# Second norm by halves with the sample between its pairs, first activations loaded among the up tiles, two more key/query buffers and another place for a table in the set-up

## The chip, the core and the metric

The kernel runs on one core of one Trainium2 chip. What counts is the time on the device, in microseconds (us), from the first to the last instruction and what lies around them. TensorE (PE) multiplies matrices, VectorE (DVE), ScalarE (ACT) and GpSimd (POOL) do the rest, SyncE (SP) issues most transfers (DMA). Each engine takes its own instructions strictly in their order; between engines an instruction can wait for others by semaphores.

## The reference, cut to what matters

One layer of a streaming encoder over 1024 prompt rows and 32 sample rows of width 1024, in float32.

```python
xn = rmsnorm(h, norm_mix)
proj = xn @ w_in
u_a, u_b, v_b, q, k, v, gates = jnp.split(proj, IN_SPLITS, axis=-1)
y_a = s5_mixer(u_a, ...)              # diagonal state space model
y_b = sgu_mixer(u_b, v_b, ...)        # layernorm, then a triangular 128x128 product
y_c = stick_breaking(q, k, v, ...)    # causal attention, 8 heads of 64
g = jax.nn.sigmoid(gates)
h = h + (g0 * (y_a @ w_branch_a) + g1 * (y_b @ w_branch_b) + g2 * (y_c @ w_branch_c)) @ w_out
xn2 = rmsnorm(h, norm_ffn)
gate, up = jnp.split(xn2 @ w_gate_up, 2, axis=-1)
h = h + (jax.nn.silu(gate) * up) @ w_down     # hidden width 2816
y = rmsnorm(h, norm_final)
```

## The kernel before

Each float32 factor is kept as a high and a low part (`hi`, `lo`), and a product is made of three matmuls, hi·hi, hi·lo and lo·hi (`mm3`, lines 144 to 146). The parts are made by ACT (a copy that rounds) and by POOL or DVE (the rest). The stages follow one another in the profiled execution thus: first norm, values, keys and queries and the set-up of the state space model to 170 us; the spatial gating (`sgu`) to 260; the state space model (`s5_main`) and attention to 650; gates and the output projection of half 0 to 780, gates of half 1 to 932; output projection of half 1 beside the second norm of half 0 to 999; the first two up tiles beside the second norm of half 1 to 1071; the other up tiles (22 in all, each 128 columns of gate and of up) to 1487; the down product in groups of two tiles from 1499 to the end.

A scheduler puts the instructions of each engine in order, by priorities and its own costs. Only TensorE in the part that starts with `out_proj(1, ...)` and ends with chunk 0 of up tile 1 keeps the order of the code (`tc.manual_schedule`).

The places that the change touches:

- `qk_dense` makes keys and queries of a pair of heads in pieces of 512 or 272 columns. ACT writes the high part of a piece into a buffer `qe` (L326), a copy into `k32` (L329), DVE the low part (L330), and SP stores `qe` to DRAM (L332). There are two buffers. Each key is also turned by TensorE and copied out by ACT (`kt`, L307).
- `s5_setup` builds tables; one of them, `KK`, is copied by 16 transfers into a matrix `D` (L632). `KK` lies in a buffer named `big`; the pool that holds it is closed after the set-up, and `sgu` puts its tiles in the same place, its `vb` (L377) where `big` was. So `vb` waits for the transfers.
- `out_proj(half, ...)` runs over four quarters of 256 columns and, in each, over the blocks of 128 rows; in half 1 the 32 sample rows (block 8) come last. After each second quarter ACT sums the squares of the block (L1168).
- `norm2(chunk, ...)` is a generator that stands beside other work: each `yield` lets the caller put a block or a product on TensorE. It takes the reciprocal roots of all blocks at once (`rstd_all`, thirteen small rows on DVE with the sum ahead), multiplies a block's 1024 columns by the norm's weights on POOL (L1213) and by the root on ACT (L1214), turns it on TensorE (L1202), and makes seven operands of a pair of blocks (L1221, L1222). The last, for the sample, comes after both pairs.
- `up_tile(i, ...)` takes seven products of a tile's weights and the operands. The weights are loaded (`raw`), combined and split by `up_weights` (ACT L1285; POOL or DVE L1286). The results go to `act_d`, one tensor in DRAM.
- `load_act(gr)` loads two tiles of `act_d` for a group of the down product (`ra`, L1401) and splits them (ACT L1402, POOL L1403, DVE L1404). It is called after all up tiles, and the loads of `h` (`hd0`, `hd1`) stand behind it.

Of the kernel before, what the change touches and what calls it, by code (L numbers as in the profile page):

```python
# [16 lines left out]
TP, TS = 1024, 32  # L17
# [31 lines left out]
def trunk_kernel(ctx: ExitStack, tc: tile.TileContext,  # L49
# [154 lines left out]
    with ExitStack() as ph1:  # L204
# [86 lines left out]
        def qk_dense(wk, hp):  # L291
# [22 lines left out]
            for which in (1, 0):  # L314
                unit = next_unit(768 + 512 * which + 128 * hp)
                dst = (q_d, k_d)[which][hp]
                for h, o, n, t0 in CHUNKS:
# [7 lines left out]
                    qe = wk.tile([128, 2, 512], F32R, name="qe", bufs=2)  # L325
# [95 lines left out]
        def s5_setup(pl, keep, out):  # L421
# [185 lines left out]
            KK = pl.tile([32, 8, 128], F32, name="KK", tag="big")  # L607
# [425 lines left out]

        qk_tasks = [qk_dense(qk, hp) for hp in range(4)]
        tasks.extend(qk_tasks)
        tasks.extend(gate_ahead(qk, h, m) for h in range(2) for m in range(AHEAD[h]))
        with pool("s5k", 1) as s5k:
            sgc = sgu_consts(s5k)
            with pool("s5t", 1) as s5t, pool("pv", 1) as pv:
                S = {}  # L1040
                setup = s5_setup(s5t, s5k, S)
                next(setup)
                v_dense(pv)
                next(setup)
                finish(qk_tasks[0])
                next(setup)
                finish(qk_tasks[1])
                for _ in setup:
                    pass
            with pool("sgu", 1) as sg:  # L1050
# [97 lines left out]
    def out_proj(half, mt, junk, beside=iter(())):  # L1148
        wo = w_out[0].rearrange("(k p) c -> p k c", p=128)
        for q in range(4):  # L1150
            us = tm_units(wo, 256 * q)
            for b in PAIRS[half][0] + PAIRS[half][1] + ((8,) if half else ()):
# [13 lines left out]
                if q % 2:  # L1166
                    c = slice(256 * q - 256, 256 * q + 256)
                    s.activation(junk()[0:rows], h_rows(b)[:, c], AF.Square, scale=1.0 / 32,  # L1168
                                 accum_out=ss2[0:rows, 10 * half + 5 * (q // 2) + (b % 4 if b < 8 else 4):][:, 0:1])
# [6 lines left out]
    act_d = dram.tile([FF, T], F32, name="act_d")  # L1176
# [22 lines left out]
    def turned(xb, rows, q, pt):  # L1199
        for e in range(4):  # L1200
            k = 4 * q + e
            pe.transpose(pt[:, 128 * e:128 * e + rows], xb[:, 128 * k:128 * k + 128], ident[0:rows, 0:rows])  # L1202
        return pt.rearrange("p (a b) -> p a b", b=128)[:, :, 0:rows]

    def ps_turn():
        return ps2.tile([128, 512], F32, name="ptn", tag="t2", bufs=2)

    def norm2(chunk, wk, X, gap):

        def scaled(b):  # L1210
            i, rows = b % 4 if b < 8 else 4, BLOCKS[b][1]
            xb = wk.tile([128, 1024], F32, name="xb")[0:rows]
            g.tensor_mul(xb, h_rows(b), gb[0:rows])  # L1213
            s.activation(xb, xb, AF.Copy, scale=r[0:rows, i:i + 1])  # L1214
            return xb
# [29 lines left out]
        order = [b for p in PAIRS[chunk] for b in p] + ([8] if chunk else [])  # L1245
        ss = wk.tile([128, 5], F32, name="ss5")
        v.tensor_add(ss, ss2[:, 10 * chunk:10 * chunk + 5], ss2[:, 10 * chunk + 5:10 * chunk + 10])
        r = rstd_all(wk, ss, 5)
        for j in range(2):
            xa = scaled(order[2 * j])  # L1250
            for _ in range(gap):
                yield
            x11 = turned(xa, 128, 0, ps_turn())
            x21 = turned(xa, 128, 1, ps_any())

            def second():
                xb = scaled(order[2 * j + 1])
                for _ in range(gap):
                    yield
                return [turned(xb, 128, q, ps_turn()) for q in range(2)]  # L1260

            yield from operands_of(128 * j, 128, x11, x21, second)
        if chunk:
            xs_ = scaled(8)
            sp.dma_start(h_d[chunk], H[chunk])
            for _ in range(gap):
                yield
            a0, a1 = turned(xs_, 32, 0, ps_turn()), turned(xs_, 32, 1, ps_any())
# [6 lines left out]
        else:  # L1275
            sp.dma_start(h_d[chunk], H[chunk])
# [28 lines left out]
    def up_tile(i, wk, chunks, X, weights=None, beside=iter(())):  # L1305
# [43 lines left out]
        for c in chunks:  # L1349
# [3 lines left out]
            for e, o in enumerate((sg[c], a[c])):  # L1353
                t0 = 512 * c + 256 * e
                sp.dma_start(act_d[128 * i:128 * i + 128, t0:t0 + 256], o[:, 0:256])
                if c:
                    t0 = TP + 16 * e
                    sp.dma_start(act_d[128 * i:128 * i + 128, t0:t0 + 16], o[:, 256:272])
# [6 lines left out]
    with pool("wu", 1) as wk:  # L1365
# [3 lines left out]
        NF = FF // 128  # L1369
        with tc.manual_schedule(engines={mybir.EngineType.PE}):  # L1370
            work = norm2(0, wk, X0, 2)
# [132 lines left out]
```

## Time and profile before

| | |
|---|---|
| median of 3 runs | 1771.8 us (1768.79 to 1782.83) |
| the profiled execution | 1785.0 us, its span 1783.3 us |
| TensorE busy | 1657.8 us, 93% of the span |
| DVE, ACT, POOL busy | 964.7, 603.6, 623.3 us |
| mean granted clock of TensorE | 0.964 of full speed |
| DMA | 211.57 MB, 119 GB/s over the span |

A row of a timeline gives the start and the duration of an instruction, and in brackets how long its engine stood idle ahead of it and what ended that. A row of the windows gives a stretch and the busy time of each engine in it. A granted clock of 0.50 is the lower of TensorE's two levels, 1.2 GHz, and 1.00 the upper, 2.4 GHz; a value between is a stretch with both.

### The profile page before, as it was taken

How to read it: one execution, taken by the hardware profiler on the slowest of the kernel's cores; microseconds unless marked ns; L12 is line 12 of the kernel's file. 1: busy time of each engine (PE TensorE's matmuls, PEld its weight loads, DVE VectorE, ACT ScalarE, POOL GpSimd, SP SyncE). 2: the span in 40 equal slices, each digit the busy share in tenths (PEclk: the TensorE clock that was granted, in tenths of full speed). 3: DMA queues.
4: the chain of work that ended last, by engine and by line, in shares of the span. 5: the costliest groups of instructions: out<-in, count | busy, mean ns of one | idle time of the engine just before them, and what ended most of it. 6: DMA issues, size and time to landing. Idle time of an engine off the chain costs nothing. (4 is left out here: it accounts for less than half of the span.)

```text
span 1783.3 us, 28031 instructions
## 1 busy us (share of the span) xinstructions
PE 1657.8 (93%) x10949; PEld 1502.6 (84%) x10949; DVE 964.7 (54%) x1838; ACT 603.6 (34%) x1102; POOL 623.3 (35%) x369
## 2 busy tenths in 40 slices
PE   6988999899988899999998879999999997999997
PEld 6977897677777788899998879999999996777775
DVE  7962523322699840730275656655555554765645
ACT  5322332123466632323224443333333332321114
POOL 2210221334010322534456554333333324644534
PEclk9988999699999999999999989999999998999999
DMA  7443245155766526764361222232222225422212
GB/s 222 113 128 82 85 123 132 60 161 159 190 150 163 149 78 212 242 215 143 94 206 37 98 75 66 82 98 73 73 72 79 87 88 203 145 79 90 72 36 86
DMA packets 271421, 211.57 MB, mean 119 GB/s; under 512 B 68340, under 2 KB 244504, under 8 KB 270776
## 3 DMA queue, kind: packets, MB, share of 16 engines
q1 hardware_dynamic: 242728, 194.56, 37.0%
q10 hardware_dynamic: 28560, 15.21, 2.9%
q8 instruction: 86, 1.41, 0.3%
q14 instruction: 47, 0.39, 0.1%
HBM read 153.83 MB, written 55.30 MB: 117 GB/s over the span
## 5 line engine op out<-in xcount | busy, mean ns | idle before, releaser
L118 POOL TENSOR_TENSOR wl<-raw,wh 128x1024 fp32r<-128x1024 f32 x120 | 304.6, 2544 | 747.1 <-ACT wh L117 705.9
L117 ACT ACTIVATE wh<-raw 128x1024 fp32r<-128x1024 f32 x120 | 126.5, 1057 | 320.1 <-PE p L146 151.0
L144 PE MATMUL p<-xo,wl 128*128 128x256 f32 (+1 forms) x616 | 177.2, 288 | 9.6 <-ACT xo L1221 6.3
L144 PE MATMUL p<-xo,wh 128*128 128x256 f32 (+1 forms) x616 | 178.0, 289 | 2.2 <-ACT wh L1285 2.1
L146 PE MATMUL p<-xo,wh 128*128 128x256 f32 (+1 forms) x616 | 178.1, 289 | 1.6 <-POOL wh L1286 1.6
L146 PE MATMUL p<-xo,wl 128*128 128x256 f32 (+1 forms) x616 | 177.4, 288 | 0.0
L145 PE MATMUL p<-xo,wh 128*128 128x256 f32 (+1 forms) x616 | 176.8, 287 | 0.0
L145 PE MATMUL p<-xo,wl 128*128 128x256 f32 (+1 forms) x616 | 176.4, 286 | 0.0
L144 PE MATMUL p_d<-xnh,wh 128*128 128x272 f32 (+1 forms) x464 | 157.9, 340 | 10.4 <-ACT vb L377 7.2
L146 PE MATMUL p_d<-xnh,wl 128*128 128x272 f32 (+1 forms) x464 | 155.5, 335 | 5.3 <-POOL wl L118 5.3
L145 PE MATMUL p_d<-xnl,wh 128*128 128x272 f32 (+1 forms) x464 | 155.3, 335 | 0.0
L1453 DVE TENSOR_TENSOR hd<-p,hd 128x512 f32<-128x512 f32 x160 | 107.1, 685 | 69.4 <-PE p L146 69.0
L145 PE MATMUL p<-wl,act 128*128 128x512 f32 x352 | 140.0, 398 | 2.4 <-POOL wl L118 2.4
L144 PE MATMUL p<-wh,act 128*128 128x512 f32 x352 | 139.9, 398 | 0.0
L146 PE MATMUL p<-wh,act 128*128 128x512 f32 x352 | 139.7, 397 | 0.0
L1286 POOL TENSOR_TENSOR wh<-raw,wh 128x512 fp32r<-128x512 f32 x59 | 77.6, 1317 | 147.1 <-ACT wh L1285 142.7
L1286 POOL TENSOR_TENSOR wl<-raw,wl 128x512 fp32r<-128x512 f32 x58 | 78.4, 1353 | 141.4 <-ACT wl L1285 141.4
L144 PEld LDWEIGHTS p<-xo,wl 128*128 128x128 f32 x616 | 117.7, 191 | 9.9 <-ACT xo L1221 6.4
L144 PEld LDWEIGHTS p<-xo,wh 128*128 128x128 f32 x616 | 118.4, 192 | 2.7 <-ACT wh L1285 2.3
L146 PEld LDWEIGHTS p<-xo,wh 128*128 128x128 f32 x616 | 118.1, 192 | 1.8 <-POOL wh L1286 1.8
L145 PEld LDWEIGHTS p<-xo,wh 128*128 128x128 f32 x616 | 118.7, 193 | 0.0
L145 PEld LDWEIGHTS p<-xo,wl 128*128 128x128 f32 x616 | 118.1, 192 | 0.0
(463 smaller groups left out, 4432.3 us busy)
## 6 DMA issues: line engine op xcount, KB each, us to landing
raw<-in_w_in_dram SPq DMA_DIRECT2D x66, 512.0 KB, 4.0
raw<-in_w_gate_up_dram SPq DMA_DIRECT2D x46, 512.0 KB, 4.6
ra<-act_d SPq DMA_DIRECT2D x22, 528.0 KB, 3.6
raw<-in_w_down_dram SPq DMA_DIRECT2D x22, 512.0 KB, 3.7
q<-q_d SPq DMA_DIRECT2D x64, 128.0 KB, 2.9
raw<-in_w_out_dram SPq DMA_DIRECT2D x16, 512.0 KB, 5.3
act_d<-fs SPq DMA_DIRECT2D x44, 128.0 KB, 1.7
act_d<-fa SPq DMA_DIRECT2D x44, 128.0 KB, 4.9
```

What stands on the lines that cost most here:

```text
L117: s.activation(wh, raw, AF.Copy)
L118: g.tensor_sub(wl, raw, wh.bitcast(F32))
L144: pe.matmul(ps, ah, bh, start=start, stop=False)
L145: pe.matmul(ps, ah, bl, start=False, stop=False)
L146: pe.matmul(ps, al, bh, start=False, stop=stop)
L1286: eng.tensor_sub(lo, src, hi.bitcast(F32))
L1453: v.tensor_add(hr[:, cs], ps, hr[:, cs])
```

## The change

Four edits go together.

1. While the set-up runs, `qe` comes in turn from two pools with two buffers each.
2. `KK` takes the place of the buffer `tg`, not `big`.
3. The second norm handles a block in two halves of 512 columns with two buffers. The roots are taken for each pair of blocks, in half 1 for three blocks first (the sample and the first pair). Half 1's blocks run in the order 8, 4, 6, 5, 7 in the output projection too, and the sample's operands come between the two pairs. A block is asked for three steps of TensorE ahead, and half 1's norm begins inside `out_proj`, after the third block of the last quarter.
4. `act_d` becomes 22 tensors. The first group's load stands in the loop over up tiles, after tile 19 in the code, the second's behind the loop but ahead of the down stage's pool, with the loads of `h` between.

```diff
-                    qe = wk.tile([128, 2, 512], F32R, name="qe", bufs=2)
+                    qe_turn[0] += 1
+                    qe = qe_pools[qe_turn[0] % len(qe_pools)].tile([128, 2, 512], F32R, name="qe", bufs=2)
...
-            KK = pl.tile([32, 8, 128], F32, name="KK", tag="big")
+            KK = pl.tile([32, 8, 128], F32, name="KK", tag="tg")
...
-            for b in PAIRS[half][0] + PAIRS[half][1] + ((8,) if half else ()):
+            for i, b in enumerate(ORDER[half]):
...
+                if q == 3 and i == 2:
+                    next(then, None)
...
-    act_d = dram.tile([FF, T], F32, name="act_d")
+    act_d = [dram.tile([128, T], F32, name=f"act_d{i}") for i in range(FF // 128)]
...
+    ORDER = ((0, 2, 1, 3), (8, 4, 6, 5, 7))
...
+        def roots(blocks):
+            i, n = order.index(blocks[0]), len(blocks)
+            ss = wk.tile([128, 5], F32, name="ss5", bufs=2)[:, 0:n]
+            o = 10 * chunk + i
+            v.tensor_add(ss, ss2[:, o:o + n], ss2[:, o + 5:o + 5 + n])
+            y = rstd_all(wk, ss, n)
+            for j, b in enumerate(blocks):
+                r[b] = y[:, j:j + 1]
...
-            xb = wk.tile([128, 1024], F32, name="xb")[0:rows]
-            g.tensor_mul(xb, h_rows(b), gb[0:rows])
-            s.activation(xb, xb, AF.Copy, scale=r[0:rows, i:i + 1])
+            for q in range(2):
+                c = slice(512 * q, 512 * q + 512)
+                xb = wk.tile([128, 512], F32, name="xb", tag="xh", bufs=2)[0:rows]
+                g.tensor_mul(xb, h_rows(b)[:, c], gb[0:rows, c])
+                s.activation(xb, xb, AF.Copy, scale=r[b][0:rows])
+                out.append(xb)
...
+        for j, (ba, bb) in enumerate(PAIRS[chunk]):
+            roots((8, ba, bb) if chunk and j == 0 else (ba, bb))
+            xa = scaled(ba)
+            for _ in range(3):
+                yield
...
+            yield from operands_of(128 * j, 128, x11, x21, second)
+            if chunk and j == 0:
+                yield from sample()
+        sp.dma_start(h_d[chunk], H[chunk])
...
+        with pool("wn", 1) as wn, tc.manual_schedule(engines={mybir.EngineType.PE}):
+            work, work1 = norm2(0, wn, X0), norm2(1, wn, X1)
+            out_proj(1, mB, lambda: wn.tile([128, 512], F32, name="junk2", tag="xt", bufs=2), work, work1)
...
+        with pool("wa", 1) as wa:
+            up_tile(1, wk, (1,), X, held)
+            up_tile(0, wk, (1,), X)
+            for i in range(2, FF // 128):
+                up_tile(i, wk, (0, 1), X)
+                if i == FF // 128 - 3:
+                    acts = [load_act(0, wa, hx)]
+            for half in range(2):
+                H[half] = hx.tile([128, 4, 1024], F32, name=f"hd{half}", tag="hx")
+                sp.dma_start(H[half], h_d[half])
+            acts.append(load_act(1, wa))
```

The set-up's instructions stand in the same order on all engines; what changes are the waits. On ACT, from the first `qe` of the first pair of heads on, with the semaphores that a row waits for in brackets (DMAHW are transfers; one line number less in the kernel before), the kernel before has:

```order
L326 ACTIVATE qe<-p_av 128x512 [waits PE_49]
L329 ACTIVATE k_1283<-p_av 128x512
L326 ACTIVATE qe<-p_d 128x272 [waits PE_49]
L329 ACTIVATE k_1283<-p_d 128x272
L117 ACTIVATE wh<-raw 128x1024 [waits DMAHW7_49,PE_49,Pool_49]
L326 ACTIVATE qe<-p_av 128x272 [waits DMAHW4_49,DMAHW5_49,DVE_49,PE_49]
L329 ACTIVATE k_1283<-p_av 128x272
L307 ACTIVATE kt<-p_t 128x256 [waits PE_49]
```

and the changed kernel has:

```order
L327 ACTIVATE qe<-p_av 128x512 [waits PE_49]
L330 ACTIVATE k_1283<-p_av 128x512
L327 ACTIVATE qe<-p_d 128x272 [waits PE_49]
L330 ACTIVATE k_1283<-p_d 128x272
L117 ACTIVATE wh<-raw 128x1024 [waits DMAHW7_49,PE_49,Pool_49]
L327 ACTIVATE qe<-p_av 128x272 [waits PE_49]
L330 ACTIVATE k_1283<-p_av 128x272
L307 ACTIVATE kt<-p_t 128x256 [waits PE_49]
```

The third `qe` has lost its wait for transfers and for DVE. In the same way the first `vb` of `sgu`, which waited for eight transfer semaphores and DVE, waits for nothing more in the changed kernel, and DVE's first `yt` waits for those eight.

On POOL, beside the first two up tiles, the second norm of half 1 and the tiles' weights share the engine. `xb` are blocks times the norm's weights (`h_9037` and `h_9058` are half 1 of h, `hS` the sample), `xo` are low parts of operands, `wh` and `wl` low parts of weights. Before:

```order
L1286 TENSOR_TENSOR wh<-raw,wh 128x512
L1213 TENSOR_TENSOR xb<-h_9037,gb 128x1024
L1286 TENSOR_TENSOR wl<-raw,wl 128x512 x2
L1213 TENSOR_TENSOR xb<-h_9037,gb 128x1024
L1222 TENSOR_TENSOR xo_9973<-t_10142,xo_9973 128x4x128
L1222 TENSOR_TENSOR xo_9974<-t_10146,xo_9974 128x4x128
L1286 TENSOR_TENSOR wh<-raw,wh 128x512
L1286 TENSOR_TENSOR wl<-raw,wl 128x512
L1213 TENSOR_TENSOR xb<-h_9037,gb 128x1024
L1222 TENSOR_TENSOR xo_9974<-t_10152,xo_9974 128x4x128
L1222 TENSOR_TENSOR xo_9287<-r_10077,xo_9287 128x4x128
L1286 TENSOR_TENSOR wh<-raw,wh 128x512
```

And in the changed kernel:

```order
L1309 TENSOR_TENSOR wh<-raw,wh 128x512
L1231 TENSOR_TENSOR xb<-h_9058,gb 128x512 x2
L1231 TENSOR_TENSOR xb<-hS,gb 32x512 x2
L1247 TENSOR_TENSOR xo_10045<-t_10184,xo_10045 128x4x128
L1247 TENSOR_TENSOR xo_10046<-t_10188,xo_10046 128x4x128
L1231 TENSOR_TENSOR xb<-h_9058,gb 128x512
L1247 TENSOR_TENSOR xo_10046<-t_10194,xo_10046 128x4x128
L1309 TENSOR_TENSOR wl<-raw,wl 128x512
L1247 TENSOR_TENSOR xo_9308<-r_10117,xo_9308 128x4x128
L1231 TENSOR_TENSOR xb<-h_9058,gb 128x512
L1309 TENSOR_TENSOR wl<-raw,wl 128x512
```

Blocks have become pairs of halves, the sample's stand ahead of the first pair's operands, and between two weight rows there are now eight rows for the norm.

On SP the first loads of activations stand in the changed kernel where the first tiles have just been stored (`act_d_6931` is tile 0, `act_d_6932` tile 1, and so on; the tiles' order is 1, 0, 2, 3):

```order
L1381 DMA act_d_6931<-fs 128x16
L1316 DMA raw<-in_w_gate_up_dram 128x8x128
L1378 DMA act_d_6931<-fa 128x256
L1381 DMA act_d_6931<-fa 128x16
L1316 DMA raw<-in_w_gate_up_dram 128x8x128
L1388 DMA ra<-act_d_6931 128x1056
L1388 DMA ra<-act_d_6932 128x1056
L1378 DMA act_d_6933<-fs 128x256 x2
```

Before, the first of them stood behind the last tile's last store:

```order
L1355 DMA act_d<-fa 128x256 x2
L1358 DMA act_d<-fa 128x16
L116 DMA raw<-in_w_down_dram 128x1024
L1401 DMA ra<-act_d 128x1056 x2
L1467 DMA hd_15650<-h_d_6929 128x4096
L1467 DMA hd_15652<-h_d_6930 128x4096
```

So the first group's two loads have moved from behind tile 21 to behind tile 0, and none of the other tiles' stores stands ahead of them.

## Rows read from the trace of the kernel before

**Rows 1.** The page: busy time of TensorE, share of the span, instructions

```profile
PE 1657.8 (93%) x10949; PEld 1502.6 (84%) x10949; DVE 964.7 (54%) x1838; ACT 603.6 (34%) x1102; POOL 623.3 (35%) x369
```

**Rows 2.** Waits of TensorE: for whom, us in total, times, the longest

```profile
PE p L1443 <- DVE act L1404: 12.3, 2, 11.5
PE ptn L1202 <- ACT xb L1214: 12.1, 3, 4.5
...
PE p_t L305 <- ACT kt L307: 7.0, 1, 7.0
...
PE p L144 <- DVE fs L1330: 3.3, 1, 3.3
```

**Rows 3.** Windows: stretch, its length, busy us of each engine, clock, DMA

```profile
100.00:112.00 12.00, 7.52 (x40) 7.50 (x41) 3.37 (x8) 3.15 (x9) 0.00 (x0) 0.57 0.89 223
164.00:176.00 12.00, 6.57 (x32) 6.57 (x33) 5.68 (x37) 3.74 (x16) 0.00 (x0) 0.57 0.15 28
328.00:360.00 32.00, 32.00 (x101) 24.13 (x101) 3.33 (x2) 6.56 (x10) 9.40 (x4) 0.52 0.18 50
...
950.00:1000.00 50.00, 45.49 (x379) 45.29 (x378) 25.76 (x36) 24.12 (x47) 32.99 (x19) 0.97 0.17 53
1000.00:1050.00 50.00, 31.31 (x212) 29.98 (x212) 32.07 (x59) 25.17 (x48) 34.57 (x26) 0.85 0.30 95
...
1100.00:1487.00 387.00, 387.00 (x3168) 387.00 (x3167) 225.96 (x448) 120.97 (x242) 124.45 (x93) 1.00 0.28 81
...
1487.00:1508.00 21.00, 8.73 (x26) 5.60 (x25) 6.86 (x10) 5.03 (x7) 9.59 (x5) 0.59 0.83 316
```

**Rows 4.** Timeline of ACT, DVE and SP in the set-up; DMA issues, us to landing

```profile
98.77 0.68 DVE L330 TENSOR_TENSOR qe<-k,qe 128x512 fp32r<-128x512 f32 x1
...
103.10 0.55 SPq L113 DMA_DIRECT2D raw<-in_w_in_dram  x1
...
103.47 0.40 ACT L326 ACTIVATE qe<-p_av 128x272 fp32r<-128x272 f32 x1 [12.46 <-DMA k_d<-qe]
...
112.37 1.06 ACT L117 ACTIVATE wh<-raw 128x1024 fp32r<-128x1024 f32 x1 [0.90 <-PE p_d L145]
...
raw<-in_w_in_dram SPq DMA_DIRECT2D x66, 512.0 KB, 4.0
...
k_d<-qe SPq DMA_DIRECT2D x8, 256.0 KB, 3.2
```

**Rows 5.** Timeline of SP, ACT and TensorE at the start of `sgu`

```profile
160.67 6.91 SPq L632 DMA_DIRECT2D D<-KK  x9
...
168.91 0.38 ACT L377 ACTIVATE vb<-p_d 128x256 f32<-128x256 f32 x1 [6.21 <-DMA D<-KK]
...
169.44 0.59 PE L144 MATMUL p_d<-xnh,wh 128*128 128x272 f32 x1 [7.21 <-ACT vb L377]
```

**Rows 6.** Timeline of DVE and POOL beside the first up tiles

```profile
1001.90 0.33 DVE L1247 TENSOR_TENSOR ss<-ss 128x5 f32<-128x5 f32 x1 [0.85 <-ACT junk L1168]
...
1005.80 0.17 DVE L1196 SCALAR_TENSOR_TENSOR rs_a<-rs_a 128x5 f32<-128x5 f32 x1
...
1046.19 1.26 POOL L1222 TENSOR_TENSOR xo<-r,xo 128x512 fp32r<-128x512 f32 x1 [0.26 <-ACT xo L1221]
```

**Rows 7.** Timeline of SP, POOL and TensorE at the down stage; landing of `ra`

```profile
1492.62 0.86 SPq L1401 DMA_DIRECT2D ra<-act_d  x2
...
1498.62 2.38 POOL L1403 TENSOR_TENSOR act<-ra,act 128x1024 fp32r<-128x1024 f32 x1 [7.71 <-ACT act L1402]
...
1498.83 0.69 PE L1443 MATMUL p<-wh,act 128*64 128x512 f32 x1 [11.53 <-DVE act L1404]
...
ra<-act_d SPq DMA_DIRECT2D x22, 528.0 KB, 3.6
```

**Rows 8.** Timeline of DVE: one line beside POOL's work, and alone

```profile
1014.59 1.50 DVE L1343 TENSOR_TENSOR fs<-fs,ft 128x256 f32<-128x256 f32 x1
...
1035.38 0.43 DVE L1343 TENSOR_TENSOR fs<-fs,ft 128x256 f32<-128x256 f32 x1
```

More of the change, by code (lines that the diff above doesn't have):

```diff
@@ L1049, in trunk_kernel @@
                     pass
+                qe_pools.pop()
             with pool("sgu", 1) as sg:
@@ L1146, in gates, with out_proj @@
         return mt
-    def out_proj(half, mt, junk, beside=iter(())):
+    def out_proj(half, mt, junk, beside=iter(()), then=iter(())):
         wo = w_out[0].rearrange("(k p) c -> p k c", p=128)
@@ L1243, in operands_of, with sample @@
             split(6, r11, g)
[L1245 to L1263, printed above, removed]
+        def sample():
             xs_ = scaled(8)
[L1265 to L1268, printed above, removed]
+            yield
+            yield
+            a0, a1 = turned(xs_[0], ps_turn()), turned(xs_[1], ps_any())
             def both():
@@ L1354, in up_tile, with load_act @@
                 t0 = 512 * c + 256 * e
-                sp.dma_start(act_d[128 * i:128 * i + 128, t0:t0 + 256], o[:, 0:256])
+                sp.dma_start(act_d[i][:, t0:t0 + 256], o[:, 0:256])
                 if c:
                     t0 = TP + 16 * e
-                    sp.dma_start(act_d[128 * i:128 * i + 128, t0:t0 + 16], o[:, 256:272])
+                    sp.dma_start(act_d[i][:, t0:t0 + 16], o[:, 256:272])
+    def load_act(gr, wk, p=hy):
+        act = p.tile([128, 2, 2 * T], F32R, name="act", tag="hx" if p is hx else "hy")
+        for e in range(2):
+            ra = wk.tile([128, T], F32, name="ra", tag="xb")
+            sp.dma_start(ra, act_d[2 * gr + e])
+            s.activation(act[:, e, 0:T], ra, AF.Copy)
+            g.tensor_sub(act[:, e, T + TS:2 * T], ra[:, 0:TP], act[:, e, 0:TP].bitcast(F32))
+            v.tensor_sub(act[:, e, T:T + TS], ra[:, TP:T], act[:, e, TP:T].bitcast(F32))
+        return act
     with pool("wg", 1) as wk:
@@ L1393, in trunk_kernel @@
         NG = FF // 256
-        def load_act(gr, p=hy):
-            act = p.tile([128, 2, 2 * T], F32R, name="act", tag="hx" if p is hx else "hy")
-            for e in range(2):
-                f0 = 256 * gr + 128 * e
-                ra = wk.tile([128, T], F32, name="ra", tag="xb")
-                sp.dma_start(ra, act_d[f0:f0 + 128, :])
-                s.activation(act[:, e, 0:T], ra, AF.Copy)
-                g.tensor_sub(act[:, e, T + TS:2 * T], ra[:, 0:TP], act[:, e, 0:TP].bitcast(F32))
-                v.tensor_sub(act[:, e, T:T + TS], ra[:, TP:T], act[:, e, TP:T].bitcast(F32))
-            return act
         def final_norm(b, ss):
@@ L1462, in down_groups @@
                 final_norm(*done)
-        acts = [load_act(0, hx)]
-        for half in range(2):
-            H[half] = hx.tile([128, 4, 1024], F32, name=f"hd{half}", tag="hx")
-            sp.dma_start(H[half], h_d[half])
-        acts.append(load_act(1))
         for gr in range(NG):
             if gr + 2 < NG:
-                acts.append(load_act(gr + 2))
+                acts.append(load_act(gr + 2, wk))
             if gr < NG - 2:
```

53 lines of the change are left out of this document (28 added, 25 removed).

## The prediction

> **What bounds the kernel now.** I read the page first: TensorE is busy 1657.8 of 1783.3 us [rows 1], so a change can only pay where TensorE stands still or runs at the lower clock. The view by windows shows where that isn't: in 1100 to 1487 it is busy 387.00 of 387.00 us at granted clock 1.00 [rows 3], so the twenty up tiles there can't become shorter. The waits of TensorE then give the stalls with their releasers [rows 2]. Four belong to code that the diff touches, and each ends a chain that I followed back in the timelines. After a stall the clock is low: the windows around three of them have 0.57, 0.57 and 0.59 of full clock, so half the time at the lower of the two levels, 1.2 GHz instead of 2.4 [rows 3]. I price that part as busy time times (1 - clock): 7.52 x 0.43 = 3.2 us, 6.57 x 0.43 = 2.8 us, 8.73 x 0.41 = 3.6 us.
>
> The profiled execution took 1785.0 us (span 1783.3 plus 1.7 around it), 13.2 above the median of the three runs, 1771.8. One stretch could explain it: from 328 to 360 TensorE is fully busy at 0.52 [rows 3], 32 x 0.48 = 15.4 us more than at full clock. Nothing in the diff is there; the other two runs have no trace, so this is a guess. I take the saving from 1785.0 and then shift it by -13.2.
>
> **Part A, four buffers for keys and queries: 5 us.** TensorE waits 7.0 us for ACT's `kt` [rows 2]. ACT was stuck 12.46 us at the third `qe` until 103.47, behind the first buffer's store; that buffer was finished by DVE only at 98.77, between rows of the S5 set-up, and a store of it takes 3.2 us [rows 4]. With four buffers the third and fourth need no wait, as the order shows. The third could then run when TensorE is done, some 6 to 7 us earlier. What is late next: `raw`, issued on SP at 103.10 behind the stores, which still wait for DVE; with 4.0 us to land it is there at 107.1, and ACT's `wh` from it, now at 112.37, can come 112.37 - 107.1 = 5.3 us earlier at most [rows 4]. ACT's copies of the S5 table stand behind that `wh`, and TensorE's PSUM behind those. So the bounds are 0 (all of it turns into this wait) and 7.0 + 3.2 = 10.2; I take 5, since the `wh` is the last link. More buffers add no instruction.
>
> **Part B, the set-up table KK in another place: 8.5 us.** ACT stood 6.21 us at `vb` until 168.91, for the transfers out of KK; TensorE waited 7.21 and restarted at 169.44. The nine last transfers are issued from 160.67 over 6.91 us [rows 5]. The order shows `vb` without a wait now; the sixteen transfers are waited for at DVE's first `yt`, behind the normalisation. Gain: 6.2 plus 2.8 of clock = 9.0, less 0.5 for what the normalisation still waits for. Bounds: 5 (the normalisation, DVE and ACT in turn, is the next bound) and 9.5.
>
> **Part C, second norm in halves, sample between the pairs: 18 us.** TensorE stands still 50 - 45.49 = 4.51 us in 950 to 1000 and 50 - 31.31 = 18.69 in 1000 to 1050, 23.2 in all; by clock 0.97 and 0.85 another 1.4 + 4.7 = 6.1 [rows 3]. Three waits for `xb` alone hold 12.1 [rows 2].
> The halves cost nothing: POOL's 1024 elements take 2.38, its 512 take 1.26 [rows 6, 7], so two halves are 0.14 more, but the first half leaves 1.1 earlier, and ACT and TensorE follow by halves. The roots: the root chain ran from 1001.90 to the last step at 1005.80 [rows 6], behind the very last block of out_proj, with TensorE waiting for what follows. Now it starts after the third block of the last quarter: two blocks of 24 matmuls and two products of 12 stand behind, 72 matmuls; at 387.00 us for 3168 [rows 3], 0.122 each, that is 8.8 us of cover for a chain of some 6 (4.1 of roots, then a half block on POOL and ACT). The 27 added root rows are of the small kind, 0.17 each [rows 6], 5 us of DVE, hidden in the same cover. The longest wait for `xb`, 4.5 in out_proj, goes but for half a us: operands are asked for three blocks ahead instead of two, 2.9 us more cover, and come by halves, 1.1 more.
> What is late next: tile 1's weights. Between two weight halves POOL now has eight rows of 512 by the order (five half blocks, two of them the sample's, and three remainders of operands): 8 x 1.26 = 10.1 us, while TensorE has four products, 4 x 1.47 = 5.9. So 4.2 us of wait appear there, and I leave as much again for the smaller ones at the weights after it. Idle then: 8.4 of 23.2, a gain of 14.8. Of the 6.1 of clock about half comes back: 3. Sum 18. Bounds: 8 (the sample's whole chain adds in front of pair two) and 25 (only 4 left of idle and clock together). The 3.3 us at `fs` [rows 2] stay: the next tile's `raw` decides there.
> A rule speaks against this part. When POOL works beside DVE, DVE's rows stretch: the multiplication at 1014.59 took 1.50, the same line at 1035.38 took 0.43 [rows 8]. The Trainium skill (Trainium Architecture — The Big Picture, "What this means for kernel authors") calls the port pair that DVE and GpSimd share an exclusive lock, not a split of bandwidth. By that rule a chain of small DVE rows could wait for a POOL row at every step (rival R6); the trace bears a wait out for single rows, not for a chain. Thirteen root rows beside POOL's 512-wide rows took 4.1 us in all before [rows 6]. Counting by those rows I keep 18.
>
> **Part D, the activations' DRAM tensor in 22 tiles, first loads early: 15 us.** TensorE waits 11.53 us at 1498.83, the two first loads of `act_d` having been issued at 1492.62, behind the last stores, and landing 3.6 us later, ACT and DVE behind [rows 7]. The order shows the two first loads between tiles 1 and 2, both halves of the first group in place hundreds of us before, and the second group's half too. Gain: 12.3 [rows 2] plus 3.6 of clock = 15.9; less 0.9 for whatever `wl` or PSUM is not ready to the microsecond. The early loads put two POOL rows of 2.4 [rows 7] among the up tiles 2 and 3, two more near the last ones, and as many shorter rows on ACT and DVE; there TensorE has no wait from 1100 on [rows 3]. If that cover were gone, 4 x 2.4 = 9.6 once. Bounds 10 and 16.
>
> **Sum.** 5 + 8.5 + 18 + 15 = 46.5. 1785.0 - 46.5 = 1738.5, and shifted to the median 1738.5 - 13.2 = 1725.3; I say 1726.
>
> **Rivals.**
> *R1: stalls come back as waits for tile 1's weights.* If POOL and ACT do pair one, sample and pair two one behind the other, part C is 8. 46.5 - 10 = 36.5: 1735. For it: POOL's eight multiplications. Against: TensorE's order was spread to match.
> *R2: the set-up has a second bound.* A gives 0 and B 5: 33, so 1739. For it: `raw` at 103.10 doesn't move.
> *R3: the early loads don't help, since something else starts the down stage* (the reload of h, 2 MB a half, or the weights). D gives 0: 31.5, 1740. Against: order and stores.
> *R4, slower.* The 3.3 us wait at `fs` comes from DVE standing, in order, behind the next tile's weights [rows 2]. With POOL's load later by the added casts, it could recur in every up tile from 2 to 21: 20 x 3.3 = 66 us, 1771.8 - 46.5 + 66 = 1791. It decides from 46.5 / 3.3 = 14 tiles on. Against: 387 us without a stall [rows 3].
> *R5: the stretch at 328.* If the measured median has this stretch at the lower clock, all times are 13 higher: 1739 for the forecast.
> *R6: the root chains stretch.* If each of 13 steps of the pair's chain in front of tile 0 met a POOL row, it would take 13 x 1.26 = 16.4 us, with its half block 18.2, against 8.8 of cover: 9.4 of wait, sum 37, 1735. For it: the row of 1.50. Against: the chain of 4.1.
>
> **How the numbers follow.** Forecast as summed 0.55; R1 0.16; R2 0.08; R3 0.06; R6 0.04; R5 0.09; R4 0.02. All but R4 are below 1771.8 x 0.99 = 1754. About 1% is what a measurement of this kernel can tell from no change. R5 together with R1 would come to 1748; all lower bounds (0 + 5 + 8 + 10 = 23) give 1749, and with R5 1762, inside 1%; so faster 0.91, same 0.07, slower 0.02. The range: all upper bounds, 10.2 + 9.5 + 25 + 16 = 60.7, give 1711; below, R1 and R5 together give 1748. I take 1711 to 1749.
>
> **What would show it.** A: no wait of ACT at the third `qe`, `wh` near 107. B: `vb` straight behind `kt`, TensorE restarting near 163. C: no wait for `xb` over 1 us, 8 to 9 us idle between the last blocks of out_proj and the last product of chunk 0, released by weights. D: under 1 us between the last up product and the first down matmul, clock 1.00 across. Wrong if the idle around tile 1's weights is over 15 us, or if a wait turns up in the up tiles.

## The result: 1.4% faster, less than half of what was forecast

The changed kernel took 1756.4 us (median of four runs: 1750.4, 1750.7, 1762.2, 1762.8) against 1777.3 for the kernel before (median of four on the same chip: 1768.8, 1771.8, 1782.8, 1785.0). The ratio is 0.986, with an interval of 0.981 to 0.990: 20.9 us faster where the sum said 46.5.

The runs of either kernel lie in two pairs some 12 us apart, and the gain is 20 to 21 us in each (1770.3 to 1750.5, 1783.9 to 1762.5). The profiled run of before, 1785.0, belongs to the upper pair and that of after, 1750.4, to the lower, so of the 34.6 us between them not all is the change. The difference stands where the prediction guessed it, in the state space model: the stretch from 328 to 360, at clock 0.52 before [rows 3], has 1.00 after.

The page of after, busy time of TensorE and the others (compare [rows 1]):

```profile
PE 1642.2 (94%) x10949; PEld 1489.0 (85%) x10949; DVE 974.5 (56%) x1864; ACT 603.3 (35%) x1111; POOL 626.5 (36%) x378
```

TensorE runs the same 10949 matmuls in the same order outside the norm and the blocks of half 1, so the k-th matmul of one trace can be set against the k-th of the other. This lead, in us by which after is earlier, is what the two timelines of TensorE give:

| place (time in before) | lead of after | of this part |
|---|---|---|
| first keys (94) | -0.1 | |
| set-up, behind the keys (118 to 160) | 1.9 | A: 2.0 |
| start of `sgu` (180) | 8.6 | B: 6.7 |
| behind the state space model and attention (843 to 933) | 22.4 | 13.8, of it 13.6 from 325 to 365 (the clock), not the change |
| first blocks of out_proj's half 1 (942) | 20.6 | C: -1.8 |
| tile 1 behind chunk 1 of the norm (1054) | 34.6 | C: 13.9 |
| from tile 6 to the last up product (1114 to 1486) | 28.6 | early loads: -6.0 |
| first down products (1509) | 44.4 | D: 15.8 |
| third group of the down product (1546) | 35.9 | D: -8.5 |
| last groups (1736 to the end) | 34.4 | -1.4 |

So the parts brought 2.0, 6.7, 12.1 and, with all that the early loads cost elsewhere, 1.3; the two big terms of the sum were 18 and 15.

How far such a step can be trusted shows in the later kernels below that keep all four edits. In the five of them with the same code as after up to the gates, A is 1.2 to 1.6 and B 4.0 to 7.0: the wait at `vb` is the same (2.8 to 3.1 us), but the clock from 155 to 185 is 1.00 in after and one of them and 0.89 to 0.94 in the others. Where an experiment's own edit doesn't touch a step, C is 11.6 to 13.1, the early loads cost 5.6 to 6.4, D brings 15.8 each time, and the step to the third group loses 7.4 to 9.7. So A and B are known to some 1 to 3 us; the big steps stand.

The windows of the same matmuls in both kernels show the middle of the table. Columns: stretch, its length, busy us (instructions) of PE, PEld, DVE, ACT, POOL, clock, DMA share, GB/s. Before, from the last blocks behind the gates, over out_proj and the norms, to tile 5:

```profile
923.00:942.30 19.30, 16.65 (x124) 16.24 (x123) 17.20 (x31) 3.98 (x5) 11.05 (x10) 0.91 0.48 164
942.30:1054.40 112.10, 88.85 (x680) 87.13 (x679) 61.52 (x101) 54.39 (x103) 70.55 (x46) 0.91 0.21 67
1054.40:1114.00 59.60, 56.17 (x443) 55.77 (x442) 37.45 (x66) 19.07 (x38) 24.60 (x18) 0.97 0.25 72
```

and after, the same work, and below it the stretch at 328 and the start of the down product:

```profile
900.70:921.60 20.90, 17.07 (x122) 16.82 (x121) 17.72 (x34) 5.04 (x7) 11.08 (x11) 0.84 0.43 147
921.60:1019.80 98.20, 85.97 (x680) 84.06 (x679) 61.85 (x125) 54.38 (x109) 68.99 (x53) 0.93 0.24 76
1019.80:1085.40 65.60, 59.15 (x443) 57.35 (x441) 36.54 (x66) 21.25 (x41) 30.64 (x20) 0.95 0.31 90
...
328.00:360.00 32.00, 32.00 (x149) 25.54 (x148) 14.67 (x4) 11.44 (x16) 18.03 (x7) 1.00 0.42 124
...
1445.00:1500.00 55.00, 49.05 (x263) 40.71 (x263) 31.69 (x47) 16.15 (x20) 36.45 (x18) 1.00 0.68 224
```

In the middle row idle time falls from 112.10 - 88.85 = 23.25 to 12.23, and 2.9 us of busy time go too. Ahead of it and behind it after is longer, by 1.6 and 6.0 us, and in the first down groups, in place of the one wait of 11.53 us ahead of them [rows 7], there are 5.95 us of idle time again.

### Where the time went, place by place

**Set-up.** Timelines of DVE, SP, ACT and TensorE in after (start, duration, instruction, in brackets the idle time ahead and its releaser):

```profile
98.78 0.69 DVE L331 TENSOR_TENSOR qe<-k,qe 128x512 fp32r<-128x512 f32 x1
...
99.49 3.52 SPq L333 DMA_DIRECT2D k_d<-qe  x4
...
103.45 1.77 ACTq L309 DMA_DIRECT2D out_dram<-kt  x2
105.27 0.39 ACT L307 ACTIVATE kt<-p_t 128x256 f32<-128x256 f32 x1 [8.46 <-DMA k_d<-qe]
...
105.71 0.40 PE L297 MATMUL p_t<-ident,k 128*32 128x128 f32 x1 [4.62 <-ACT kt L307]
...
111.15 1.06 ACT L117 ACTIVATE wh<-raw 128x1024 fp32r<-128x1024 f32 x1 [0.51 <-ACT kts L299]
...
160.56 2.24 ACTq L309 DMA_DIRECT2D out_dram<-kt  x4
162.85 0.38 ACT L378 ACTIVATE vb<-p_d 128x256 f32<-128x256 f32 x1 [2.05 <-DMA out_dram<-kt]
```

The third `qe` no longer waits. But ACT also issues the output of the turned keys (L309), and that issue waits, by its semaphores, for a transfer of the same store of the first `qe`, which DVE still finishes at 98.78 [rows 4: 98.77]. In the trace it waits for the very semaphore on which its own landing is then counted: the two transfers share a semaphore, not data. ACT stands 8.46 us instead of 12.46, TensorE 4.62 instead of 7.0, and `wh` comes 1.2 us earlier. The Trainium skill (DMA: Bandwidth & Descriptors, "Anatomy of one DMA — SWDGE (gpsimd) path") says, in a section on GpSimd's transfers, of DMA engines in general that they don't wait for semaphores: any such wait happens on the sequencer that issues. These rows, with ACT as the issuer, agree, since ACT's next copy starts at 105.27, behind its issues from 103.45 over 1.77 us. At `sgu`, `vb` stands 2.05 us where it stood 6.21 [rows 5], behind four such issues. They are not new; in the kernel before they stand in the same place, hidden in the longer wait:

```profile
162.46 2.05 ACTq L309 DMA_DIRECT2D out_dram<-kt  x4
```

**Sample first.** Timelines of POOL and TensorE in after:

```profile
911.34 2.50 POOL L118 TENSOR_TENSOR wl<-raw,wh 128x1024 fp32r<-128x1024 f32 x1 [1.75 <-ACT wh L117]
913.79 0.91 POOL L1148 CAST mt<-m 128x32 fp32r<-128x32 f32 x2
...
914.75 0.48 PE L132 MATMUL p<-wh,mt 128*64 128x256 f32 x1 [3.83 <-POOL mt L1148]
```

With the sample first in out_proj, TensorE needs `mt` at once, and POOL's cast stands behind a remainder of weights. That the loss of 1.8 us here is the price of it isn't shown: the kernel before with part 4 alone, where the sample is still last, loses 1.4 in the same place, and the experiment on the sample's place below gains nothing there.

**Norm and tile 1.** Waits of TensorE in after from 934 to 1100, grouped (total, times, longest):

```profile
PE p L146 <- POOL wl L1309: 3.3, 2, 3.1
PE p L144 <- DVE fs L1353: 3.2, 1, 3.2
PE p L144 <- ACT wh L1308: 2.3, 1, 2.3
PE p L146 <- POOL wh L1309: 2.2, 1, 2.2
PE ptn L1239 <- ACT xb L1232: 2.1, 2, 1.5
PE p L144 <- ACT fa L1349: 1.6, 1, 1.6
PE p L144 <- ACT wl L1308: 1.4, 1, 1.4
PE p L144 <- DVE fu L1361: 1.2, 1, 1.2
```

The waits for `xb` went from 12.1 [rows 2] to 2.1 us. Tile 1's weights took their place with 3.1 + 2.3 + 2.2 + 1.4 = 9.0.

**Tiles 2 to 5.** Timeline of SP in after:

```profile
1051.86 12.25 SPq L1388 DMA_DIRECT2D ra<-act_d  x2
```

The two early loads of activations take SP 12.25 us, and the waits for `fu` and `fa` in the list above (2.8 us) fall at 1064 and 1078.

**Start of the down product.** Timelines of SP, ACT, POOL, DVE and TensorE in after:

```profile
1475.36 17.03 SPq L1388 DMA_DIRECT2D ra<-act_d  x6
...
1469.07 1.09 ACT L1389 ACTIVATE act<-ra 128x1056 fp32r<-128x1056 f32 x1 [2.90 <-DMA ra<-act_d]
...
1488.37 1.09 ACT L1389 ACTIVATE act<-ra 128x1056 fp32r<-128x1056 f32 x1 [1.16 <-DMA ra<-act_d]
1489.37 1.99 ACT L117 ACTIVATE wh<-raw 128x1024 fp32r<-128x1024 f32 x2
1491.26 0.57 ACT L135 ACTIVATE htmp<-p 32x512 f32<-32x512 f32 x1
...
1470.51 4.74 POOL L1390 TENSOR_TENSOR act<-ra,act 128x1024 fp32r<-128x1024 f32 x2
...
1492.00 4.71 POOL L118 TENSOR_TENSOR wl<-raw,wh 128x1024 fp32r<-128x1024 f32 x2
1496.68 1.25 POOL L1475 TENSOR_TENSOR hS<-hS,htmp 32x512 f32<-32x512 f32 x1
...
1470.19 5.11 DVE L1391 TENSOR_TENSOR act<-ra,act 128x32 fp32r<-128x32 f32 x1 [2.12 <-ACT act L1389]
...
1499.32 0.50 PE L144 MATMUL p<-wh,act 128*128 128x512 f32 x1 [3.65 <-DVE htmp L136]
```

The first down matmul follows the last up product without a wait. Then the copies of six half loads of activations stand one behind the other on ACT, the first starting at 1469.07 and the last at 1488.37, most of the time waiting for their transfers, ahead of the second group's weights and of the sample's result `htmp`; POOL's six remainders stand likewise ahead of `hS`. TensorE waits 0.45, 1.82 and 3.65 us for results to be taken out of PSUM.

### The profile page after: what moved, and what is told of

It reads as the page before. It is cut to its first block, busy times and chain, and to the rows that moved or that the text cites. A ratio compares the mean times of both kernels' runs of the same rounds, so it can differ in the third digit from the quotient of the medians.

```text
span 1748.7 us, 28070 instructions
## 1 busy us (share of the span) xinstructions
PE 1642.2 (94%) x10949; PEld 1489.0 (85%) x10949; DVE 974.5 (56%) x1864; ACT 603.3 (35%) x1111; POOL 626.5 (36%) x378
```

## The experiments

Each was compared with the kernel before on the same chip; leads are read as in the table above.

### Which parts carry the gain

Part 3 alone; as a diff against the changed kernel, whose other parts go back to those of the kernel before:

```diff
-            KK = pl.tile([32, 8, 128], F32, name="KK", tag="tg")
+            KK = pl.tile([32, 8, 128], F32, name="KK", tag="big")
...
-                qe_pools.append(pv)
...
-    act_d = [dram.tile([128, T], F32, name=f"act_d{i}") for i in range(FF // 128)]
+    act_all = dram.tile([FF, T], F32, name="act_d")
+    act_d = [act_all[128 * i:128 * i + 128, :] for i in range(FF // 128)]
...
+        acts = [load_act(0, wk, hx)]
```

> The kernel before with the edits of the second norm alone (halves, sample between the pairs, roots per pair); `qe`, `KK` and the loads of the activations as before. In the changed kernel TensorE was 37.6 us ahead of before in tile 2 and 28.6 in tile 5: it gave back 9.0. Theory W: the weights of tiles 2 to 4 set that pace, whatever else stands there. Then this kernel gains 13 to 15 by the end of chunk 0 and gives back 6 or more; net 5 to 9 us. Theory L: the early load of the first activations delays SP, POOL and DVE there (SP stands 12.25 us at the second `ra`). Then it gives back less than 4; net 10 to 14 us.

1770.5 us, ratio 0.993 [0.989, 0.997], against 1782.7: 12.2 us. The lead rises from 2.6 (nothing of this part is ahead of it) to 16.6 behind the norm, 14.0 us, and is still 16.5 at tile 6: nothing is given back among the up tiles. Where the loads of activations come late, TensorE has one wait from 1049 to the last up product, the known one at `fs`, and the old one at the down product:

```profile
1071.51 0.39 PE L144 MATMUL p<-xo,wl 128*128 128x272 f32 x1 [2.87 <-DVE fs L1352]
...
1483.62 0.69 PE L1463 MATMUL p<-wh,act 128*64 128x512 f32 x1 [12.82 <-DVE act L1390]
```

So the loss in tiles 2 to 5 isn't the norm's. Part 4 alone, on the kernel before (the norm's tiles in a pool of their own, to make room):

```diff
-    act_d = dram.tile([FF, T], F32, name="act_d")
+    act_d = [dram.tile([128, T], F32, name=f"act_d{i}") for i in range(FF // 128)]
...
+                if i == NF - 3:
+                    acts = [load_act(0, wa, hx)]
...
+            acts.append(load_act(1, wa))
```

> The kernel before with the activations in 22 tensors and the early loads alone (the second norm's tiles get a pool of their own, since the early loads need its room; its order is as before). Both theories: TensorE gains 15 to 16 us at the first down product and loses 6 to 9 of them in the first two groups, where ACT, POOL and DVE stand in six loads in a row; net 7 to 9 there. Theory W: no new waits in tiles 2 to 5 beside the 3.3 us of before. Theory L: waits of 2 to 4 us in tiles 3 to 5, and half clock after them, so that the net is 3 to 6.

1778.4 us, ratio 0.999 [0.995, 1.003]. Its lead goes from -2.4 at 1054 to -6.1 at 1119 (3.7 lost), to 9.7 at the first down products (15.8 gained), and to 2.2 by the third group (7.6 lost), 0.7 at the end. The two longest waits in that third step, on TensorE's timeline:

```profile
1523.07 0.57 PE L144 MATMUL p<-wh,act 128*128 128x512 f32 x1 [1.89 <-DVE hd L1459]
1534.54 0.50 PE L144 MATMUL p<-wh,act 128*128 128x512 f32 x1 [2.66 <-DVE htmp L136]
```

Part D in itself moves the wait away and loses most of its gain again in two other places.

The changed kernel without the two added buffers:

```diff
-                qe_pools.append(pv)
...
-                qe_pools.pop()
```

> The changed kernel without its first edit (two buffers `qe` again). By the comparison of the changed kernel and before the four buffers gained 2.0 to 2.9 us in front of the spatial gating, of 6.99 waited. Theory S: the wait is 6.99 again instead of 4.62, and 1 to 3 us are lost, the clock included; all else stays. If the buffers did more than that, 4 or more are lost.

1760.6 us, ratio 0.988 [0.979, 0.996]; the wait at `kt` is 6.97 us again, and the kernel is 2.0 us behind after from 113 to 160. But 1.1 of this it was behind at 94 already, ahead of the third `qe`. From 94 on its own gain over before is 1.1 us, against 1.2 to 2.0 in the kernels with four buffers: the buffers by themselves are worth 1 us at most, less than the change's comparison said.

### The wait in the set-up

The remainder of a key or query on POOL instead of DVE during the set-up, so that the store can leave earlier:

```diff
-                    v.tensor_sub(qe[:, 1, 0:n], full, qe[:, 0, 0:n].bitcast(F32))
+                    (g if which and len(qe_pools) > 1 else v).tensor_sub(qe[:, 1, 0:n], full, ...)
```

> The changed kernel, with the low part of the keys of the set-up made on POOL, which has nothing to do there, and not on DVE. Theory S: the 4.62 us that TensorE still waits at 105.71 come from the same late store of the first keys as before; only the row that waits for it has changed (ACT's second issue of `kt`, done 7 us late). The keys are then finished 8 us earlier, the wait falls below 1 us, and the clock with it: 5 to 7 us gained up to the next stage. Rival: the loads of weights behind on SP (raw, 103.10) set the pace; then the wait stays over 3 us.

The wait of 4.62 us is gone; TensorE is 7.3 us ahead of after from 112 to 160, as the theory has it, and 4.7 at 250. (From 160 on kernels with the same code differ by up to 3 us, as said at the table.) ACT's `wh` then stands at

```profile
103.09 1.06 ACT L117 ACTIVATE wh<-raw 128x1024 fp32r<-128x1024 f32 x1 [0.93 <-PE p_d L145]
```

8.1 us earlier than in after, where it starts at 111.15. The time, 1751.8 us (0.986 [0.978, 0.993]), can't show 5 us with four runs; the trace does. The cause of the first wait was DVE's late remainder. The same edit on the kernel before, with its two buffers:

```diff
-                    v.tensor_sub(qe[:, 1, 0:n], full, qe[:, 0, 0:n].bitcast(F32))
+                    (g if which and in_setup[0] else v).tensor_sub(qe[:, 1, 0:n], full, ...)
```

> The kernel before, with nothing but the low part of the set-up's keys made on POOL and not on DVE; still two buffers. Theory S: what TensorE waits for at 104.5 is that DVE finishes the first keys at 98.8; without that the 6.99 us are gone with two buffers too, 7 to 9 us up to the next stage. Rival: two buffers are too few; then a wait of 3 us or more stays at the third `qe`.

1781.5 us, ratio 0.998 [0.994, 1.002]. The wait of 7.0 us is gone here too, and TensorE is 9.5 us ahead of before at 112, but only 2.9 at 119, where 7 to 9 were expected:

```profile
108.91 0.40 ACT L326 ACTIVATE qe<-p_d 128x272 fp32r<-128x272 f32 x1 [5.04 <-DMA q_d<-qe]
...
109.85 1.97 PE L580 MATMUL p_z<-ident,big 128*128 128x128 f32 x8 [4.45 <-ACT BT L581]
```

Now the buffers do bind, at a later `qe` than the third, as the rival had it, and ACT's copies of the table `BT` behind it keep TensorE. From 94 to 130 the remainder on POOL alone gains 3.2 us on before and the buffers alone 1.2 to 2.0; together, in the changed kernel, 9.8, more than the two apart.

### The loads among the up tiles

Two theories for the 6.0 us: SP stands at the second load, since there is one buffer `ra`, and with it the weights; or the loads' casts take ACT, POOL and DVE while tiles 2 to 5 need them. Two buffers:

```diff
-        with pool("wa", 1) as wa:
+        with pool("wa", 2) as wa:
```

> The changed kernel with two buffers instead of one for the early loads `ra`, so that SP needn't stand 12.25 us at the second load ahead of the next tile's weights. Norm alone gave back 3.4 us in tiles 2 to 4, with the early loads 9.0; the loads alone lost 4.2 there. Theory SP: the loss is SP's, whose stores and weights come late behind the second load; then TensorE gains 4 to 6 us up to tile 6. Theory E: it is the place of the loads' rows on POOL, ACT and DVE among the weights' rows; then it gains less than 2.

SP no longer stands (the two issues take 0.80 us), but after's lead over this kernel grows from 1.4 at 1049 to 2.9 at tile 6:

```profile
1064.27 0.39 PE L144 MATMUL p<-xo,wl 128*128 128x256 f32 x1 [1.62 <-DVE fu L1361]
1068.38 0.59 PE L144 MATMUL p<-xo,wl 128*128 128x272 f32 x1 [2.41 <-DVE fu L1361]
```

The first theory falls. That the casts, sooner in the queues, come at a worse moment is an argument, not shown apart. (In the first down groups this kernel loses 4.6 us where after loses 8.5, and it ends 1.2 ahead of after.) Other loads instead: the down product takes groups 8 and 9 first, whose activations exist only late, so nothing can be loaded among tiles 2 to 5:

```diff
+    GO = (8, 9, 0, 1, 2, 3, 4, 5, 6, 7, 10)
...
-                    acts = [load_act(0, wa, hx)]
+                    acts = [load_act(GO[0], wa, hx)]
...
-            acts.append(load_act(1, wa))
+            acts.append(load_act(GO[1], wa))
...
-                acts.append(load_act(gr + 2, wk))
+                acts.append(load_act(GO[gr + 2], wk))
...
```

> The changed kernel with another order of the down groups: tiles 16 to 19 first, then 0 to 15, then 20 and 21. The first group's loads can then only be issued when tile 17 is stored, not after tile 0. The sums come out the same but for rounding. Theory P: what the early loads cost is a matter of place, since tiles 2 to 4 have no weights in hand; late in the up stage they cost under 1 us, and 4 to 6 us are gained up to tile 6, with the gain at the down stage kept within 2 us. Rival M: the cost moves with the loads to tiles 18 to 21; the sum gains less than 2.

1747.5 us, ratio 0.979 [0.971, 0.987]. Against after TensorE gains 5.5 us between tile 1 and tile 6, and no wait comes up in the later tiles. The other half of theory P missed: 3.0 us are lost again in the first down groups, where TensorE waits 8.0 us and in after 5.9, so 2.4 are kept. The same stretch of after and of this kernel, 1049 to 1100, in the windows; after:

```profile
1049.00:1100.00 51.00, 44.78 (x335) 43.59 (x334) 30.14 (x52) 16.24 (x32) 21.11 (x13) 0.93 0.39 115
```

late groups first:

```profile
1049.00:1100.00 51.00, 47.92 (x380) 47.73 (x379) 31.60 (x58) 16.48 (x34) 16.69 (x13) 0.97 0.30 85
```

380 matmuls instead of 335, and POOL 4.4 us less busy. The loads at that place are the cause of the loss; through which engine they act isn't shown.

### The start of the down product

Theory: the six half loads in a row are what holds the evacuation. One place of `hy` is kept occupied until the third group, so that only four follow one another:

```diff
+        hold = hy.tile([128, 2, 2 * T], F32, name="hold", tag="hy")
+        v.memset(hold[:, 0, 0:8], 0.0)
         for gr in range(NG):
+            if gr == 2:
+                tmp = late.tile([32, 512], F32, name="htmp")
+                v.tensor_copy(tmp[:, 0:8], hold[0:32, 0, 0:8])
```

> The changed kernel with one of the four places for activations kept empty until the second down group (a small write and a small read of eight columns are added), so that four loads instead of six stand in a row ahead of ACT's `htmp`. Theory Q: the three waits in the first groups (0.45, 1.82, 3.65 us, and what the clock loses) come from ACT and DVE standing in their order behind loads that only the third and fourth group need. Then the last of them, 3.65, is gone, and 4 to 7 us are gained. Rival: the transfers' rate at the start of the down stage sets the pace; then the waits stay, or move by less than 1 us.

1748.9 us, ratio 0.984 [0.977, 0.992]. Against after TensorE gains 7.9 us between the first and the third group, more than the 4 to 7 expected. All of TensorE's waits from 1460 to 1560:

```profile
PE p L144 <- DVE hd L1481: 0.3, 1, 0.3
```

The theory holds: two loads less ahead of `wh` and `htmp` suffice. A copy less there is also a transfer less, and this run doesn't part the two.

### Sample and roots

The sample third in the order, as the last of the first three blocks:

```diff
-    ORDER = ((0, 2, 1, 3), (8, 4, 6, 5, 7))
+    ORDER = ((0, 2, 1, 3), (4, 6, 8, 5, 7))
...
-            roots((8, ba, bb) if chunk and j == 0 else (ba, bb))
+            roots((ba, bb, 8) if chunk and j == 0 else (ba, bb))
```

> The changed kernel with the sample third instead of first in the output projection's second half (order 4, 6, 8, 5, 7). TensorE waits 3.83 us at 914.75 for POOL's casts of the sample's rows. Theory F: that wait is the price of the sample first; blocks 4 and 6 cover it: it falls below 1 us, and with the clock 3 to 6 us are gained by block 7 of the first quarter, kept to the end within 2. Rival: the wait is for the gates' last results as such; then block 4 waits instead, 2 to 4 us.

1759.7 us (0.986 [0.971, 1.000]). The rival holds: the wait of 3.83 goes, and two shorter ones, of 1.42 and 1.60 us, come back, which also the kernel before has there (1.05 and 1.60). Up to the first quarter's last block it gains 0.2 us on after; the sample first costs next to nothing. It gains 1.3 more beside the norm, where kernels with no edit to it differ by 1.5. The two shorter waits:

```profile
933.59 0.39 PE L144 MATMUL p<-wh,m 128*128 128x256 f32 x1 [1.42 <-ACT m L1142]
935.70 0.58 PE L146 MATMUL p<-wh,m 128*128 128x256 f32 x1 [1.60 <-DVE m L1143]
```

The roots of the second pair right behind those of the first:

```diff
-            roots((8, ba, bb) if chunk and j == 0 else (ba, bb))
+            if not (chunk and j):
+                roots((8, ba, bb) if chunk else (ba, bb))
...
-            for _ in range(3):
+            for k in range(3):
                 yield
+                if chunk and j == 0 and k == 0:
+                    roots(PAIRS[1][1])
```

> The changed kernel with the roots of blocks 5 and 7 taken three steps of TensorE earlier, before the sample's operands. In the changed kernel that chain of thirteen small DVE rows lasted from 989.1 to 1005.7, 16.7 us, since most rows took 0.95 to 1.24 us beside POOL's work, not 0.17. Theory R: the chain sets when the second pair's operands come, and 2 to 4 us are gained by the end of chunk 0. Rival: tile 1's weights set the pace there; the chain shrinks or moves and TensorE gains less than 1.

1749.6 us, ratio 0.980 [0.972, 0.988]. In the trace it gains 1.4 us on after between 976 and 1012, but the kernel with the late groups, which has no edit there, gains 1.2: nothing clear of the spread, so the rival holds. In after this chain lasted 16.7 us, from 989.06 to the end of the row at 1005.57. Its twelve rows behind the sum took 9.8 of them, and other rows of DVE stood between. A row stretches until POOL's row beside it ends:

```profile
1003.69 1.28 POOL L1309 TENSOR_TENSOR wl<-raw,wl 128x512 fp32r<-128x512 f32 x1
1003.78 1.20 DVE L1202 SCALAR_TENSOR_TENSOR rs_a<-rs_a 128x2 f32<-128x2 f32 x1
...
1005.57 0.16 DVE L1202 SCALAR_TENSOR_TENSOR rs_a<-rs_a 128x2 f32<-128x2 f32 x1
```

Its stretch costs little, since TensorE waits for tile 1's weights there (2.33 us at 999.88, 2.17 at 1002.55).

### All of it together

The changed kernel with the POOL remainder, the late groups first, the held place, the sample third and the early roots:

> The changed kernel with five further edits: low parts of the set-up's keys on POOL, tiles 16 to 19 as the first down groups, one of the four places for activations empty until the second group, the sample third, and the roots of blocks 5 and 7 earlier. If the causes found apart are apart: 4 to 5 us at the set-up, 5 in tiles 2 to 5, 6 to 9 in the first down groups, 1 to 2 each for the sample and the roots; 17 to 21 us less than the changed kernel, 38 to 42 less than before. If late loads and the empty place hinder each other at the down stage, 8 to 12 less than the changed kernel.

1734.4 us (median of six), against 1784.2 for the kernel before: ratio 0.974 [0.968, 0.980], 2.6% faster where the change alone is 1.4%. The ratio makes 46 us less than before, more than the 38 to 42 expected. In the trace it is ahead of after by 7.6 us at 160, 11.1 at 1039, 17.4 at tile 6 and 25.3 from the third down group on; 1723.4 us of span against 1748.7. The late loads and the empty place don't hinder each other: from the first to the third down group it loses 0.7 us, where after loses 8.5. More than half of what TensorE still waits from 900 to 1100 is for tile 1's weights: 3.50 and 1.17 us for `wh`, 3.09 and 1.97 for `wl`.

## Why the prediction was right or wrong

The direction was right, the size wrong: the range began at 1711 and ended at 1749, and the median is 1756.4.

- **Base and shift.** The guess on the stretch at 328 was right, and R5 with it: in the 13 traces it has clock 0.52 to 0.71 in the seven executions from the upper times of their kernel and 1.00 in the six others, with and without the change. But a shift to 1771.8 took the base as a run of the lower pair, while the median over more runs lies between the pairs. Of the miss of 31.1 us (1756.4 - 1725.3), 5.5 are this (1777.3 - 1771.8), and the rest, 25.6, is the sum, 46.5 against 20.9.
- **A, 5 expected, 2.0 measured (1.2 to 2.0 over six executions).** The step that failed is "the third and fourth need no wait": true of `qe`, but ACT's queue holds its own transfers, and one of them, the second pair of issues of `kt`, waited for the same store. The kernel without the added buffers has a step of 1.1 here, so at most 1 us is theirs. The order of ACT's issues with their semaphores would have shown it. What is late next was not `raw` but `kt`, and `wh` came 1.2 us earlier (112.37 to 111.15), not up to 5.3.
- **B, 8.5 expected, 6.7 measured.** The wait that goes was right. "Less 0.5 for what the normalisation still waits for" was mis-sized: 2.05 us on ACT and 3.1 on TensorE remain, behind the four issues of `kt` that the trace of before had at 162.46. The bounds, 5 and 9.5, held in this execution; in two of five others with the same code the step was 4.0 and 4.1.
- **C, 18 expected, 12.1 measured, 12.2 alone by the medians.** The mis-sized term is "Idle then: 8.4 of 23.2": 12.23 of 23.25 are left. Tile 1's weights alone hold 9.0 of them; the clock gave back 2.9, with 3 forecast. Not seen were the rest of the waits (2.1 for `xb`, 1.2 for `xo`), 12.23 - 9.0 = 3.2 us, and a loss of 1.8 at out_proj's first blocks, whose cause stays open. The bound of 8 held.
- **D, 15 expected, 1.3 measured.** This is the largest miss. "Gain 15.9" was right (15.8). Two sentences failed. "There TensorE has no wait from 1100 on", used as cover for the early loads: the first group's loads came at 1052 and their copies up to 1071, in the tiles ahead of that stretch, where weights and operands still came from the same engines; 6.0 us, about half of them waits and the rest clock. And "less 0.9 for whatever `wl` or PSUM is not ready", which puts what the loads of the third and later groups do at next to nothing: with two groups in place, six half loads stand in a row as the down stage opens, ahead of the first evacuations of PSUM; 8.5 us. The prediction asked what releases the first matmul and not what the queue holds behind it.
- **The last 1.4 us.** Near the end the two waits for weights are the same in both kernels, 1.30 and 1.1 us, but the clock of after is 0.91 from 1683 to 1702 where before has 1.00 in the same work. It isn't the change's doing: three later kernels with all four edits lose nothing here against before, and the kernels before with part 3 or part 4 alone lose 1.4 and 1.5.
- **Rivals.** R1's mechanism, weights of tile 1, came at the size that the sum had already. R2 half came: another bound in the set-up (with A at 0 and B at 5 its sum is 38, not 33). R3 named the wrong link: the first product did start early. R4 did not come as said; waits came in the first few tiles, not in twenty. R6's stretched chain came, at the second pair and without a price that the traces show; the chain in front of tile 0, 970.66 to 973.84 with POOL at rest for most of it, took 3.2 us. No rival had a cost of the loads behind the wait that they remove.
- **Two readings.** "Thirteen root rows beside POOL's 512-wide rows took 4.1 us" was put against R6, but POOL stood idle from 1003.45 on, and the one row that lay beside its row stretched to that row's end:

```profile
1002.17 1.28 POOL L1286 TENSOR_TENSOR wh<-raw,wh 128x512 fp32r<-128x512 f32 x1
1002.27 1.22 DVE L1190 TENSOR_SCALAR rs_a<-ss 128x5 f32<-128x5 f32 x1
```

  So the trace of before spoke for the stretch. And a mean clock of 0.57 is not "half the time at the lower" level but (1 - 0.57) / 0.5 = 0.86 of it; the price, busy time times (1 - clock), doesn't hang on that.

## What to carry to other kernels

When a transfer or a load is moved ahead, price not only the wait it ends but each queue at the place it goes to, and what the freed buffers let the next loads do: here both together took 14.5 of 15.8 us. An added buffer helps only if no other instruction of the same engine waits for the same event; look for the late producer (here DVE's remainder) before the buffer. The two together gained more than the sum of each alone. Before a step of a microsecond or two is put down to an edit, look at the same step in kernels that lack the edit.

## What the runs showed of the hardware

- A subtraction of 32 columns on DVE took 5.11 us beside two POOL rows that took 4.74 us, and 0.17 us with POOL at rest; a root row of two columns took 1.20 beside POOL and 0.16 without it. The Trainium skill (Trainium Architecture — The Big Picture, "What this means for kernel authors") calls the ports that DVE and GpSimd share an exclusive lock; these rows agree, since each long one ends with POOL's: the row of 5.11 us, from 1470.19, ended only with the second of the two POOL rows, from 1470.51 to 1475.25. Why it lost to rows that started after it, the traces don't show.
- The stretch from 328 to 360, with TensorE busy throughout in both, ran at clock 0.52 in before and 1.00 in after, with 101 and 149 matmuls; no edit is near it. A kernel with all four edits (one place kept empty) has 0.59 there, and the kernel before with POOL's remainder alone 1.00. What decides it stays open.
